# Down projection of an encoder's feed-forward block: one product of full size against seven products of half size

## The chip, the cores and the metric

One core of one Trainium2 chip runs the kernel. The metric is the device time of a run in microseconds (us); lower is better. Engines are named as in the profile: PE (TensorE's matmuls), PEld (its weight loads), DVE (VectorE), ACT (ScalarE), POOL (GpSimd), SP (the engine whose queue issues most DMAs).

## The reference, cut to what matters

The layer is a mixer (attention heads and recurrent heads) followed by a gated feed-forward block. The change is in the last of these, for T = 768 tokens (512 of `x_sample`, then 256 of `x_prompt`), D = 1024, D_FF = 2816, all float32:

```python
def _conv_ffn(xn, w_gate, w_up, conv_w, conv_b, w_down):
    a = xn @ w_gate
    a = lax.conv_general_dilated(a, conv_w[:, None, :], ...) + conv_b   # depthwise, 3 taps along the tokens
    b = xn @ w_up
    return (jax.nn.gelu(a, approximate=True) * b) @ w_down              # <- the down projection

# y = h + RMSNorm_post2(_conv_ffn(RMSNorm_pre2(h), ...))
```

## The kernel before

A product in float32 precision is made from three float32r matmuls: each operand is split into a high part (an ACT copy, line 242) and a low part (a DVE subtraction, line 243; helper `split_to`), and hi·hi, lo·hi and hi·lo are added in PSUM.

**Gate and up.** The gate and up projections are already made by seven half-size products (the names P1 to P7; A11, A12, ... are halves of the tokens' operand, B11, ... halves of the weights). A pair p is a column tile f and its partner f + 11 of one of the two weight matrices (even p gate, odd p up). For every pair `prep` makes the weights' combinations (line 828, DVE) and splits them, six products ahead of `product` (line 844, 12 matmuls of 384 columns for each product). `keep` and `collect` take the results out of PSUM into CG (gate) or CU (up), `gate` runs the convolution and GELU into UM, and `gated` multiplies by up (line 895) and stores the gated tile of 128 features to `Gd` in DRAM (lines 896 and 897, SP). Weights come through a ring of five raw buffers (RAW and EX), loaded at line 228 on SP.

**Down.** `run` ends with the down projection, out of `Gd` and `w_down`. It has two halves of 512 output columns. In each, for each f of 22 feature tiles, six token tiles of 128 take three matmuls of 512 columns (line 1149): 2 x 22 x 6 x 3 = 792. One PSUM bank holds one token tile. Gated tiles are loaded (line 1122, 384 KB each, every one twice) into four buffers in X and split three tiles ahead into XN2; weights are loaded in pieces of 512 KB and split. The last f's (4 in the first half, 6 in the second) run token tile by token tile, so that each token tile's norm (lines 1173 to 1176 in the first half, 734 to 737 in the second), residual (line 1185) and store (line 1187) lie beside the next tile's matmuls, but for the last one.

**What sets the order.** SP's and POOL's instructions run in the order of the program. Those of PE, DVE and ACT are ordered by the scheduler when the program is built, and each engine then runs its list in order.

Of the kernel before, what the change touches and what calls it, by code (L numbers as in the profile page):

```python
# [6 lines left out]
F32 = mybir.dt.float32  # L7
# [3 lines left out]
OP = mybir.AluOpType  # L11

D = 1024
# [29 lines left out]
H = T // 2  # L43

# [48 lines left out]
class Encoder:  # L93
# [80 lines left out]
    def weight_list(self):  # L174
# [27 lines left out]
        wd = a["w_down"][0].rearrange("(k p) c -> p k c", p=128)  # L202
        for half in range(2):
            for s in range(NF // 2):
                L.append((wd[:, s:s + NF // 2 + 1:NF // 2, 512 * half:512 * half + 512], 2, 512))
# [608 lines left out]
    def prep(self, upto):  # L814

        nc = self.nc
        while self.n_op < min(upto + 1, len(self.prods)):
# [13 lines left out]
            if kind == "P4":  # L831
                self.n_split = n + 2
                self.load(n + 7)

# [58 lines left out]
    def gated(self, f, c, u):  # L893
        nc = self.nc
        nc.vector.tensor_tensor(self.v(u, T + 1), self.v(u, T + 1), self.v(c, T + 1), op=OP.mult)
        nc.sync.dma_start(self.Gd[f, :, 0:SA], self.v(u, SA))
        nc.sync.dma_start(self.Gd[f, :, SA:T], self.v(u + SA + 1, SB))

    def run(self):
        nc, ps = self.nc, self.ps  # L900
        self.weight_list()
        self.Gd = self.tc.dram_tile([NF, 128, T], F32, name="gd")
        self.Hd = self.tc.dram_tile([T, D], F32, name="hd")
# [114 lines left out]
        for f in range(7):  # L1018
# [10 lines left out]
            if f == 0:  # L1029
# [8 lines left out]
                                                   ("S3", self.X + 16 * H))}  # L1038

# [67 lines left out]

        n1 = N_FFN + 2 * NF
        order = [f + x for f in range(NF // 2) for x in (0, NF // 2)]
        GS, GR, HR = self.XN2, self.X + 9216, self.X  # L1110
        M0, M1 = self.V, self.V + 3072
        banks = ((0, 3, 5, 6, 7, 2), (1, 4, 0, 3, 5, 6))
        LATE = (4, 6)
        n_l = n_g = 0

        def gs(n):
            return GS + 1536 * (0, 1, 4, 5, 2, 3)[n % 6]

        def gload(upto):
            nonlocal n_l  # L1120
            while n_l < min(upto, 2 * NF):
                nc.sync.dma_start(self.v(GR + T * (n_l % 4), T), self.Gd[order[n_l % NF]])
                n_l += 1

        def gsplit(upto):
            nonlocal n_g
            while n_g < min(upto, 2 * NF):
                gload(n_g + 1)
                o = gs(n_g)
                self.split_to(o, o + T, GR + T * (n_g % 4), T)  # L1130
                n_g += 1
                gload(n_g + 4)

        for m in range(4, len(self.prods)):
            self.prep(m)
            self.product(m)
            self.keep(m)
            p, kind = self.prods[m]
            if p == NF - 1:
                {"P1": lambda: gload(4), "P6": lambda: (gsplit(2), self.split(n1 + 1)), "P3": lambda: gsplit(4),  # L1140
                 "P7": lambda: self.split(n1 + 2)}.get(kind, lambda: None)()
            self.collect(m)
            self.prep(m + 6)
        def down(half, f, i):
            m = n1 + 11 * half + f // 2
            wh, wl = self.hi(m) + 512 * (f % 2), self.lo(m) + 512 * (f % 2)
            o = gs(half * NF + f)
            for go, wo_, first, last in ((o, wh, True, False), (o + T, wh, False, False), (o, wl, False, True)):
                nc.tensor.matmul(ps[:, banks[half][i], :], self.r(go + 128 * i, 128), self.r(wo_, 512),  # L1149
                                 start=(f == 0 and first), stop=(f == NF - 1 and last))  # L1150

        ss0 = {}
        self.split(n1 + 4)
        for half in range(2):
            late = NF - LATE[half]
            for f in range(late):
                gsplit(half * NF + f + 3)
                for i in range(NTT):
                    down(half, f, i)
                if f % 2:  # L1160
                    self.split(n1 + 11 * half + f // 2 + 4)
            if half == 0:
                for i in range(NTT):
                    nc.sync.dma_start(self.v(HR + 1024 * i, 1024), self.Hd[128 * i:128 * i + 128, :])
            gsplit((half + 1) * NF)
            for i in range(NTT):
                for f in range(late, NF):
                    down(half, f, i)
                out = ps[:, banks[half][i], :]
                h, m0 = HR + 1024 * i, M0 + 512 * i  # L1170
                if half == 0:
                    ss = self.col()
                    nc.scalar.activation(self.v(self.JUNK, 512), out, AF.Square, accum_out=ss)
                    nc.vector.tensor_tensor(self.v(m0, 512), out, self.v(self.WB, 512), op=OP.mult)
                    ss0[i] = self.col()
                    nc.vector.tensor_scalar(ss0[i], ss, D * EPS, None, op0=OP.add)
                    if i == 2:
                        gsplit(NF + 2)
                    continue
                m1 = M1 + 512 * (i % 4)  # L1180
                rs = self.post_stats(ss0[i], out, self.v(m1, 512))
# [42 lines left out]
```

## Time and profile before

| | |
|---|---|
| median of 3 runs | 1028.98 us (1028.87 to 1029.11) |
| the profiled execution's own time | 1028.98 us |
| its span (first to last instruction) | 1027.2 us |
| mean clock granted to TensorE | 0.992 of full speed |
| PE busy | 996.8 us, 97% of the span |
| DVE busy, ACT busy | 651.8 us, 498.3 us |
| gate and up products, without the first four | 524 to 840.5 us of the span |
| down projection's matmuls | 840.5 to 1020.2 us |

Read it from the top: the engine that is busy nearly always, then the stretch of the span in which each part of the program runs, then what each of the other engines does in that stretch. The profiled execution lasted as long as the median run, and 1.8 us of its time lie outside the span. A matmul's duration in the profile is longer than the distance to the next one, since matmuls are pipelined; busy time divided by count gives the distance.

### The profile page before, as it was taken

The page shows a single profiled execution, that of the slowest core. Times are in us where ns is not written, and L with a number is a line of the kernel's source. Part 1 is how long each engine was busy: PE and PEld are TensorE (multiplying, and loading weights), DVE is VectorE, ACT ScalarE, POOL GpSimd, SP SyncE. Part 2 cuts the span into 40 slices and gives each one's busy share as a digit, 9 for nine tenths or more (in the row PEclk, how much of TensorE's full clock was granted, in tenths as well). Part 3 has the DMA queues.
Part 4 walks back from the last instruction along what each step waited for, and adds up shares of the span by engine and source line. Part 5 has one row for each costly group of instructions (what it writes and reads, how often), then busy time and mean ns, then how long its engine had stood idle before and what let it go on. Part 6 is the DMA issues. An engine that isn't in the chain of part 4 may idle for free.

```text
span 1027.2 us, 17503 instructions
## 1 busy us (share of the span) xinstructions
PE 996.8 (97%) x7087; PEld 888.9 (87%) x7087; DVE 651.8 (63%) x1106; ACT 498.3 (49%) x901; POOL 49.4 (5%) x45
## 2 busy tenths in 40 slices
PE   5999999999989999999979999999999999999997
PEld 5988888888878777779879999999999998888885
DVE  5445949494623677636899777887777673345334
ACT  4363535252414889735656455555544563334321
POOL 1100000000022011001100000000000000000001
PEclk9999999999989999999989999999999999999999
DMA  9041111111024122142345233233332466474313
GB/s 276 24 124 44 43 42 42 42 43 42 3 69 119 44 58 57 29 144 83 129 121 151 74 112 97 74 104 107 113 113 75 137 223 212 153 276 156 132 41 123
DMA packets 109874, 104.01 MB, mean 101 GB/s; under 512 B 4602, under 2 KB 89698, under 8 KB 109794
## 3 DMA queue, kind: packets, MB, share of 16 engines
q1 hardware_dynamic: 108930, 101.33, 31.9%
q10 hardware_dynamic: 864, 1.57, 0.4%
q8 instruction: 55, 0.90, 0.4%
q14 instruction: 25, 0.20, 0.1%
HBM read 85.58 MB, written 14.94 MB: 98 GB/s over the span
## 4 chain that ended last, share of the span: by engine, by line
PE 86%; issue 6%; DVE 3%; ACT 2%; POOL 1%; DMA 1%; SPq 0%; DVEq 0%; POOLq 0%; ACTq 0%
PE ps L844 31%; PE ps L338 19%; PE ps L1149 17%; PE ps L710 4%; PE ps L346 4%; PE ps L430 2%; PE ps L630 2%; PE ps L663 2%; PE ps L652 2%; PE ps L515 1%; DMA RAW<-w_in 1%; PE ps L512 1%; DVE XN L796 1%; DVE V L747 0%; POOL sm L526 0%
## 5 line engine op out<-in xcount | busy, mean ns | idle before, releaser
L338 PE MATMUL ps<-X,W 128*128 128x512 f32 (+1 forms) x1200 | 232.5, 345 | 0.0
L338 PEld LDWEIGHTS ps<-X,W 128*128 128x128 f32 x1200 | 187.2, 190 | 28.0 <-issue 2.4
L844 PE MATMUL ps<-XN,W 128*128 128x384 f32 x1056 | 189.8, 337 | 5.4 <-ACT XN L795 4.6
L844 PEld LDWEIGHTS ps<-XN,W 128*128 128x128 f32 x1056 | 184.9, 189 | 6.4 <-ACT XN L795 5.4
L1149 PE MATMUL ps<-W,XN 128*128 128x512 f32 x792 | 179.7, 389 | 0.0
L1149 PEld LDWEIGHTS ps<-W,XN 128*128 128x128 f32 x792 | 148.7, 188 | 30.8
L242 ACT ACTIVATE W<-RAW 128x1024 fp32r<-128x1024 f32 (+1 forms) x92 | 79.7, 869 | 175.9 <-PE ps L338 75.6
L844 PE MATMUL ps<-X,W 128*128 128x384 f32 x792 | 144.2, 340 | 0.0
L844 PEld LDWEIGHTS ps<-X,W 128*128 128x128 f32 x792 | 140.8, 189 | 0.0
L243 DVE TENSOR_TENSOR W<-RAW,W 128x512 fp32r<-128x512 f32 (+1 forms) x82 | 78.1, 955 | 66.0 <-ACT W L242 65.9
L242 ACT ACTIVATE W<-V 128x512 fp32r<-128x512 f32 x88 | 55.1, 628 | 59.0 <-PE ps L844 56.0
L243 DVE TENSOR_TENSOR W<-V,W 128x512 fp32r<-128x512 f32 x88 | 59.8, 688 | 17.8 <-ACT W L242 17.7
L346 PE MATMUL ps<-W,X 128*128 128x256 f32 (+1 forms) x432 | 66.6, 312 | 3.3 <-ACT X L804 2.5
L346 PEld LDWEIGHTS ps<-W,X 128*128 128x128 f32 x432 | 61.7, 196 | 4.9 <-ACT X L804 3.1
L243 DVE TENSOR_TENSOR XN<-X,XN 128x768 fp32r<-128x768 f32 x44 | 41.8, 955 | 35.8 <-ACT XN L242 35.7
L242 ACT ACTIVATE XN<-X 128x768 fp32r<-128x768 f32 x44 | 36.8, 840 | 42.8 <-PE ps L1149 42.6
L710 PE MATMUL ps<-W,X 128*128 128x512 f32 (+1 forms) x288 | 57.2, 343 | 0.0
L710 PEld LDWEIGHTS ps<-W,X 128*128 128x128 f32 x288 | 44.1, 188 | 6.9 <-issue 1.6
L242 ACT ACTIVATE W<-EX 128x512 fp32r<-128x512 f32 (+1 forms) x34 | 25.3, 745 | 47.5 <-PE ps L1149 22.5
L243 DVE TENSOR_TENSOR W<-EX,W 128x512 fp32r<-128x512 f32 (+1 forms) x34 | 28.2, 830 | 29.6 <-ACT W L242 29.6
L304 POOL TENSOR_TENSOR sm<-sm 128x1 f32<-128x1 f32 x24 | 15.2, 639 | 622.1 <-DVE sm L735 587.7
L860 ACT ACTIVATE V<-ps 128x384 f32<-128x384 f32 x66 | 31.4, 475 | 6.3 <-PE ps L844 6.3
(183 smaller groups left out, 1151.8 us busy)
## 6 DMA issues: line engine op xcount, KB each, us to landing
X<-gd SPq DMA_DIRECT2D x44, 384.0 KB
RAW<-w_in SPq DMA_DIRECT2D x32, 512.0 KB
RAW<-w_gate SPq DMA_DIRECT2D x14, 512.0 KB
RAW<-w_up SPq DMA_DIRECT2D x13, 512.0 KB
RAW<-w_down SPq DMA_DIRECT2D x13, 512.0 KB
gd<-UM SPq DMA_DIRECT2D x22, 256.0 KB
EX<-w_up SPq DMA_DIRECT2D x9, 512.0 KB
EX<-w_down SPq DMA_DIRECT2D x9, 512.0 KB
```

The source lines that it names most:

```text
L242: nc.scalar.activation(self.r(hi, n), self.v(src, n), AF.Copy)
L243: (eng or nc.vector).tensor_tensor(self.r(lo, n), self.v(src, n), self.v(hi, n), op=OP.subtract)
L338: nc.tensor.matmul(out, self.r(wo + 128 * k, 128), self.r(xo + T * k + t0, tn), start=(k == 0 and first), stop=(k == NK - 1 and last))
L346: self.nc.tensor.matmul(out, self.r(xo + T * k + 128 * i, 128), self.rap(wo + 128 * k, [[1024, tiles], [1, 128]]), start=(k == 0 and first ...
L430: nc.tensor.matmul(ps[64 * cb:64 * cb + 64, b + h, 64 * c:64 * c + 64], self.v(kt + t0, 64, *HALF[h]), qv(t0, h), start=True, stop=True)
L630: nc.tensor.matmul(ps[:, 4 + h, 0:L], self.r(QS + T * h + t0 + 128 * i, 128), self.r(x + T * h + t0, L), start=z, stop=not z)
L652: nc.tensor.transpose(ps[:, 6 + h, 128 * kt:128 * kt + 128], ms(j, n, h)[:, 128 * kt:128 * kt + 128], self.ident)
L663: nc.tensor.matmul(o[64 * h:64 * h + 64], self.v(vb + 128 * kt + 64 * h, 64), self.v(pt(s, h) + L * kt, L), start=kt == 0, stop=kt == L // ...
L710: nc.tensor.matmul(out, self.r(mo + T * f + 128 * i, 128), rhs, start=(f == 0 and first), stop=(f == NK - 1 and last))
L844: nc.tensor.matmul(out, self.r(wo + 128 * k, 128), self.r(xo + H * k, H), start=kind in BEGINS and k == 0 and first, stop=k == 3 and last, ...
L860: self.nc.scalar.activation(self.v(o, H), self.ps[:, self.pair_banks(p)[BANK_OF[kind]], 0:H], AF.Copy)
L1149: nc.tensor.matmul(ps[:, banks[half][i], :], self.r(go + 128 * i, 128), self.r(wo_, 512), start=(f == 0 and first), stop=(f == NF - 1 and ...
```

## The change

The down projection is made the way gate and up are made: the token half (384 tokens), the feature half (11 tiles) and the column half (512) are combined so that seven products of half size in each dimension replace eight. `UNITS` lists 77 units in four stages of 22, 22, 22 and 11: (P1, P5), (P6, P3), (P7, P2), (P4), one unit for each product and feature tile f of 11. A unit is 3 token tiles x 3 matmuls of 512 columns (line 1012): 77 x 9 = 693. Banks are kept from stage to stage (P6, P7 and P4 add to what P1 left there, P3 to what P5 left), so that a stage's result is copied out (line 1071, ACT) or added to a block in V (line 1050, DVE) where it ends.

The tokens' sums (S1 to S4) are made where the gated tiles are made, in `token_sums`: for each f below 11, seven DVE instructions (lines 912 to 917) and six stores to a new DRAM tensor `Sd`. The second halves of those `Gd` tiles are no longer stored. Gated operands are loaded as 192-KB pieces (line 960, six buffers), weights as 256-KB pieces (line 949, ten buffers, and eleven places in X for B12, which is first copied from `w_down` to a DRAM tensor `Bd`, line 835, one piece for each second pair). `down_prep` works six units ahead and subtracts weights on DVE (lines 985, 991, 996) in 44 of the 77 units.

```diff
+UNITS = [(k, f) for ks in (("P1", "P5"), ("P6", "P3"), ("P7", "P2"), ("P4",)) for f in range(NS) for k in ks]
...
             if kind == "P4":
                 self.n_split = n + 2
                 self.load(n + 7)
+                if p % 2:
+                    nc.sync.dma_start(self.Bd[p // 2], self.wd[:, p // 2, 512:1024])
...
-        nc.sync.dma_start(self.Gd[f, :, 0:SA], self.v(u, SA))
-        nc.sync.dma_start(self.Gd[f, :, SA:T], self.v(u + SA + 1, SB))
+        nc.sync.dma_start(self.Gd[f, :, 0:H], self.v(u, H))
+        if f >= NS:
+            nc.sync.dma_start(self.Gd[f, :, H:SA], self.v(u + H, SA - H))
+            nc.sync.dma_start(self.Gd[f, :, SA:T], self.v(u + SA + 1, SB))
+        else:
+            self.token_sums(f, u, self.UM + NG * ((2 * f + 1) % 4), c, c + NG)
+
+    def token_sums(self, f, a1, a2, c0, c1):
...
+        for o, t, m in pieces:
+            nc.vector.tensor_tensor(self.v(s1 + t, m), self.v(a1 + o, m), self.v(a2 + o, m), op=OP.add)
+        nc.vector.tensor_tensor(self.v(s2, H), self.v(s1, H), self.v(a1, H), op=OP.subtract)
+        for o, t, m in pieces:
+            nc.vector.tensor_tensor(self.v(c0 + o, m), self.v(a1 + t, m), self.v(a1 + o, m), op=OP.subtract)
+        for o, t, m in pieces:
+            nc.vector.tensor_tensor(self.v(c1 + o, m), self.v(a2 + t, m), self.v(s2 + t, m), op=OP.subtract)
+        nc.sync.dma_start(self.Sd[f, :, 0:H], self.v(s1, H))
...
+    def down_prep(self, upto, cap=1000):
...
+            src, x, y = {"P5": (t, 0, 1), "P7": (self.V + 3072 + 1024 * (f % 3), 0, 1)}.get(k, (None,) * 3)
+            if k == "P6":
+                src = t
+                nc.vector.tensor_tensor(self.v(t, 512), self.v(raw[0], 512), self.v(t, 512), op=OP.subtract)
...
+            w, g = self.down_ops(u)
+            self.split_to(w, w + 4096, src, 512)
+            self.split_to(g, g + H, self.X + 9216 + H * (u % 6), H)
+            if k == "P2":
+                nc.vector.tensor_tensor(self.v(t, 512), self.v(raw[0], 512), self.v(t, 512), op=OP.subtract)
...
+            self.down_g(u + 7)
...
+    def down_product(self, u, tiles):
...
+        for i in tiles:
+            for go, wo, first, last in ((g, w, True, False), (g + H, w, False, False), (g, w + 4096, False, True)):
+                nc.tensor.matmul(self.down_bank(k, i), self.r(go + 128 * i, 128), self.r(wo, 512),
...
+    def down(self):
...
+        late = 6
...
+        for u in range(n - late):
+            k, f = UNITS[u]
+            self.down_prep(u)
+            self.down_product(u, range(N))
+            if f == NS - 1:
+                if k in ("P1", "P5", "P6"):
+                    for i in range(N):
+                        nc.scalar.activation(self.down_block(*{"P1": (i, 0), "P5": (i + N, 1), "P6": (i, 1)}[k]),
+                                             self.down_bank(k, i), AF.Copy)
+                else:
+                    for i in range(N):
+                        add(*{"P3": (i, 1), "P7": (i + N, 1), "P2": (i, 0)}[k], k)
...
+            self.down_prep(u + 6)
...
+        for i in range(N):
+            for u in range(n - late, n):
+                self.down_product(u, (i,))
...
+            out = self.down_bank("P4", i)
+            rs = self.rsqrt(self.down_square(i + N, 0, out, ss[i + N]))
+            self.down_weigh(i + N, 0, out)
+            self.down_store(i + N, rs)
```

**DVE beside gate and up**, from the second gated product of a tile f to the next use of new raw weights (W is the split weights, CU and UM the up and gated tiles, V the combined weights). Before:

```order
L895 TENSOR_TENSOR UM<-UM,CU 128x769 [waits DVE_49,Activation_49]
L243 TENSOR_TENSOR W<-V,W 128x512 [waits PE_49,Activation_49] x2
L828 TENSOR_TENSOR V<-EX,RAW 128x512 [waits DMAHW7_49,DMAHW4_49]
L243 TENSOR_TENSOR W<-RAW,W 128x512 [waits PE_49,Activation_49]
L828 TENSOR_TENSOR V<-EX,V 128x512 [waits DVE_49]
```

and in the changed kernel:

```order
L897 TENSOR_TENSOR UM<-UM,CU 128x769 [waits DVE_49,Activation_49]
L912 TENSOR_TENSOR CU<-UM 128x128 [waits DVE_49]
L912 TENSOR_TENSOR CU<-UM 128x256
L915 TENSOR_TENSOR CU<-UM 128x128
L913 TENSOR_TENSOR CU<-CU,UM 128x384 [waits DVE_49]
L915 TENSOR_TENSOR CU<-UM 128x256
L917 TENSOR_TENSOR CU<-UM,CU 128x128 [waits DVE_49]
L917 TENSOR_TENSOR CU<-UM,CU 128x256
L243 TENSOR_TENSOR W<-V,W 128x512 [waits PE_49,Activation_49] x2
L243 TENSOR_TENSOR W<-RAW,W 128x512 [waits PE_49,Activation_49]
```

The seven sums stand in one block ahead of the next low parts.

**SP at the same place**: the stores of the gated tile and the loads of weights that are queued behind them. Before:

```order
L896 DMA gd<-UM 128x512 [waits DMAHW2_49,DVE_49]
L897 DMA gd<-UM 128x256 [waits DMAHW3_49]
L228 DMA EX<-w_gate 128x8x128 [waits DMAHW4_49,Activation_49]
L228 DMA EX<-w_up 128x8x128 [waits DMAHW5_49]
L228 DMA RAW<-w_up 128x8x128 [waits DMAHW6_49,DVE_49]
```

and in the changed kernel:

```order
L898 DMA gd<-UM 128x384 [waits DMAHW5_49,DVE_49]
L918 DMA sd<-CU 128x384 [waits DMAHW6_49,DVE_49]
L919 DMA sd<-CU 128x384 [waits DMAHW7_49,DVE_49]
L922 DMA sd<-CU 128x128 [waits DMAHW0_49]
L922 DMA sd<-CU 128x256 [waits DMAHW1_49,DVE_49]
L922 DMA sd<-CU 128x128 [waits DMAHW2_49,DVE_49]
L922 DMA sd<-CU 128x256 [waits DMAHW3_49,DVE_49]
L228 DMA RAW<-w_gate 128x8x128 [waits DMAHW4_49,Activation_49]
L228 DMA EX<-w_up 128x8x128 [waits DMAHW5_49]
```

Six stores in place of one now wait for DVE ahead of the weights' loads.

**DVE in the down projection**, between two weight splits of one half before (XN_4144 holds the split gated operands, X the raw ones):

```order
L243 TENSOR_TENSOR W<-RAW,W 128x1024 [waits PE_49,Activation_49]
L243 TENSOR_TENSOR XN_4144<-X,XN_4144 128x768 [waits DMAHW7_49,Activation_49]
L243 TENSOR_TENSOR XN_4144<-X,XN_4144 128x768 [waits DMAHW1_49,Activation_49]
L243 TENSOR_TENSOR W<-RAW,W 128x1024 [waits PE_49,Activation_49]
L243 TENSOR_TENSOR XN_4144<-X,XN_4144 128x768 [waits DMAHW2_49,Activation_49]
```

and in the third stage of the changed kernel, one unit of P2 and one of P7 (X also holds B12, V and UM the weights' differences):

```order
L243 TENSOR_TENSOR W<-RAW,W 128x512 [waits PE_49,Activation_49]
L243 TENSOR_TENSOR XN_4145<-X,XN_4145 128x384 [waits DMAHW3_49,Activation_49]
L243 TENSOR_TENSOR W<-V,W 128x512 [waits PE_49,Activation_49]
L243 TENSOR_TENSOR XN_4145<-X,XN_4145 128x384 [waits DMAHW5_49,Activation_49]
L991 TENSOR_TENSOR V<-RAW,X 128x512 [waits DMAHW2_49,DVE_49]
L996 TENSOR_TENSOR UM<-RAW,UM 128x512 [waits DMAHW0_49]
```

One round was three subtractions for 36 matmuls; it is six smaller ones for 18.

## Rows read from the trace of the kernel before

**Rows 1.** The page: span, busy time of PE, and the chain that ended last

```profile
span 1027.2 us, 17503 instructions
PE 996.8 (97%) x7087; PEld 888.9 (87%) x7087; DVE 651.8 (63%) x1106; ACT 498.3 (49%) x901; POOL 49.4 (5%) x45
...
PE 86%; issue 6%; DVE 3%; ACT 2%; POOL 1%; DMA 1%; SPq 0%; DVEq 0%; POOLq 0%; ACTq 0%
```

**Rows 2.** Groups of the page: line, count, busy us, mean ns

```profile
L1149 PE MATMUL ps<-W,XN 128*128 128x512 f32 x792 | 179.7, 389 | 0.0
```

**Rows 3.** Busy time in stretches: columns, gate and up, down, the end

```profile
core 0: us, PE busy (x) PEld busy (x) DVE busy (x) ACT busy (x) POOL busy (x), PEclk, DMA share, GB/s
524.00:840.50 316.50, 316.50 (x1799) 316.50 (x1799) 250.88 (x400) 173.12 (x309) 0.00 (x0) 0.99 0.39 117
840.50:1020.20 179.70, 179.70 (x794) 148.54 (x792) 75.25 (x92) 57.81 (x81) 2.75 (x5) 1.00 0.45 158
880.00:920.00 40.00, 40.00 (x178) 33.15 (x177) 15.06 (x16) 13.36 (x17) 0.00 (x0) 1.00 0.58 207
1020.20:1027.20 7.00, 0.04 (x1) 0.00 (x0) 2.22 (x4) 0.69 (x2) 0.55 (x1) 0.82 0.30 112
```

**Rows 4.** Groups by shape, 420 to 1028 us: nearest to the added work

```profile
L243 DVE TENSOR_TENSOR W<-V,W 128x512 fp32r<-128x512 f32 x88 | 59.8, 688 | 17.8 <-ACT W L242 17.7
L242 ACT ACTIVATE W<-V 128x512 fp32r<-128x512 f32 x88 | 55.1, 628 | 59.0 <-PE ps L844 56.0 <-DVE V L828 3.0
L860 ACT ACTIVATE V<-ps 128x384 f32<-128x384 f32 x66 | 31.4, 475 | 6.3 <-PE ps L844 6.3
L880 DVE TENSOR_TENSOR CU<-ps,V 128x384 f32<-128x384 f32 x22 | 12.2, 556 | 4.1 <-PE ps L844 4.1
L880 DVE TENSOR_TENSOR CU<-ps,V 128x256 f32<-128x256 f32 x11 | 4.6, 416 | 0.0
L880 DVE TENSOR_TENSOR CU<-ps,V 128x128 f32<-128x128 f32 x11 | 3.2, 292 | 7.4 <-PE ps L844 7.4
```

**Rows 5.** Waits of PE, then ACT, 524 to 1028 us: total, times, longest

```profile
PE ps L844 <- DVE XN L796: 0.7, 1, 0.7
...
ACT W L242 <- PE ps L844: 104.1, 94, 1.5
```

**Rows 6.** Busy time in stretches beside gate and up, columns as in 3

```profile
531.00:546.00 15.00, 15.00 (x88) 15.00 (x87) 14.39 (x24) 12.28 (x21) 0.00 (x0) 1.00 0.59 173
561.00:576.00 15.00, 15.00 (x88) 15.00 (x87) 14.62 (x24) 8.38 (x15) 0.00 (x0) 1.00 0.27 75
681.00:711.00 30.00, 30.00 (x173) 30.00 (x173) 23.10 (x38) 16.00 (x30) 0.00 (x0) 1.00 0.37 105
```

**Rows 7.** Timeline, 705 to 732 us: start, us, engine, instruction [idle before]

```profile
724.53 0.96 DVE L895 TENSOR_TENSOR UM<-UM,CU 128x769 f32<-128x769 f32 x1
726.00 0.69 DVE L243 TENSOR_TENSOR W<-V,W 128x512 fp32r<-128x512 f32 x1 [0.51 <-ACT W L242]
728.14 0.69 DVE L243 TENSOR_TENSOR W<-V,W 128x512 fp32r<-128x512 f32 x1 [1.45 <-ACT W L242]
730.64 0.69 DVE L828 TENSOR_TENSOR V<-EX,RAW 128x512 f32<-128x512 f32 x1 [1.81 <-DMA EX<-w_gate]
...
726.41 0.40 SPq L228 DMA_DIRECT2D EX<-w_gate  x1
```

**Rows 8.** Timeline of PE, 505 to 531 us, and busy time behind its wait

```profile
522.52 0.44 PE L844 MATMUL ps<-XN,W 128*128 128x384 f32 x1 [4.56 <-ACT XN L795]
...
524.00:528.00 4.00, 4.00 (x14) 4.00 (x14) 3.82 (x7) 1.67 (x4) 0.00 (x0) 0.50 0.12 30
```

**Rows 9.** DMA issues of the page into X and of w_down: count, KB

```profile
X<-gd SPq DMA_DIRECT2D x44, 384.0 KB
...
RAW<-w_down SPq DMA_DIRECT2D x13, 512.0 KB
...
EX<-w_down SPq DMA_DIRECT2D x9, 512.0 KB
```

More of the change, by code (lines that the diff above doesn't have):

```diff
@@ L43 @@
 H = T // 2
+NS = NF // 2
+UNITS = [(k, f) for ks in (("P1", "P5"), ("P6", "P3"), ("P7", "P2"), ("P4",)) for f in range(NS) for k in ks]
 TILES = (0, 1, 3, 2, 4, 5)
@@ L201, in weight_list @@
                     L.append(cols(src, 128 * x))
[L202 to L205, printed above, removed]
         self.wl = L
@@ new lines, in down_setup @@
+    def down_setup(self):
+        self.n_dp = self.n_dg = self.n_dw = self.n_used = 0
+        self.raws = [("B12", 0), ("B11", 0), ("B11", 1), ("B11", 2)]
+        for f in range(1, NS):
+            self.raws += [("B12", f)] + ([("B11", f + 2)] if f + 2 < NS else [])
+        self.raws += [("B22", f) for f in range(NS)]
+        for f in range(NS):
+            self.raws += [("B22x", f), ("B21", f)]
+        ring = [x for x in self.raws if x[0] != "B12"]
+        self.ring = {x: i for i, x in enumerate(ring)}
@@ new lines, in raw_at, with down_w @@
+    def raw_at(self, x):
+        if x[0] == "B12":
+            return self.X + (11520 if x[1] == 0 else 512 * (x[1] - 1))
+        i = (4 * NF + self.ring[x]) % 10
+        return (self.RAW + 1024 * ((N_FFN + i // 2) % 3) if i < 6 else self.EX + 1024 * (i // 2 - 3)) + 512 * (i % 2)
+    def down_w(self, upto):
+        while self.n_dw < min(upto, len(self.raws)):
+            x = self.raws[self.n_dw]
+            k, c = {"B11": (0, 0), "B21": (NS, 0)}.get(x[0], (NS, 1))
+            self.nc.sync.dma_start(self.v(self.raw_at(x), 512), self.Bd[x[1]] if x[0] == "B12" else
+                                   self.wd[:, k + x[1], 512 * c:512 * c + 512])
+            self.n_dw += 1
@@ L1106, in run @@
         self.collect(3)
[L1108 to L1134, printed above, removed]
+        self.down_setup()
+        n = len(self.prods)
+        for m in range(4, n):
             self.prep(m)
@@ L1137, in run @@
             self.keep(m)
[L1138 to L1141, printed above, removed]
             self.collect(m)
             self.prep(m + 6)
[L1144 to L1181, printed above, removed]
-                y = self.a["y_sample"][0, 128 * i:128 * i + 128] if i < 4 else \
-                    self.a["y_prompt"][0, 128 * (i - 4):128 * (i - 4) + 128]
-                for c, src, eng in ((0, m0, nc.sync), (512, m1, nc.scalar)):
-                    nc.vector.scalar_tensor_tensor(self.v(src, 512), self.v(src, 512), rs, self.v(h + c, 512),
-                                                   op0=OP.mult, op1=OP.add)
-                    eng.dma_start(y[:, c:c + 512], self.v(src, 512))
-            if half == 0:
-                self.split(n1 + 11 + 4)
@@ L1191, in bcast @@
+            if m == n - 6:
+                self.down_g(6)
+                self.down_w(4)
+            if m >= n - 6:
+                self.down_prep(m + 6 - n, {n - 6: 4, n - 5: 14}.get(m, 1000))
+        self.down()
     def bcast(self, name):
```

98 lines of the change are left out of this document (added).

## The prediction

> **What bounds the kernel now.** First the page: PE is busy for 996.8 of 1027.2 us and holds 86% of the chain that ended last [rows 1]. Then the groups, for what the down projection is made of: 792 matmuls of line 1149 in 179.7 us, 0.2269 us from one to the next, with no idle time ahead of them [rows 2]. Then busy time in stretches, for what the other engines have to spare in each part. Beside gate and up PE is busy all the time and DVE for 250.88 of 316.5 us; in the down projection PE is busy for 179.70 of 179.70 us, DVE for 75.25, ACT for 57.81, the 16 DMA engines for 0.45 of it [rows 3]. Last the waits: PE waits once for DVE there, 0.7 us, while ACT waits for PE 94 times, 104.1 us in all, since the next place in the ring of split weights is still in use [rows 5]. So in both parts PE alone sets the pace and the preparation runs as far ahead as its buffers let it. A matmul taken out here shortens the span by its distance, for as long as the preparation keeps up.
>
> **What is taken out.** 792 matmuls become 77 x 9 = 693 of the same shape and in the same pattern, three for a token tile with the high part loaded twice. 99 x 0.2269 = 22.5 us less; the down projection would last 693 x 0.2269 = 157.2 us. The Trainium skill (TensorE: Matmul & The Clock Gate, section "Wait — 56ns, not 53.3ns?") gives a warm matmul of N columns N / 2.4 GHz and some 2.5 ns, which would be 215.8 ns for 512 and an estimate of 21.4 us for the 99; the trace has 226.9 ns, and the row decides.
>
> **What is added beside gate and up.** For each f of 11, seven DVE sums: three of 128 elements, three of 256, one of 384. The nearest rows are line 880's 292, 416 and 556 ns [rows 4]: 3 x 0.292 + 3 x 0.416 + 0.556 = 2.68 us, 29.5 us for eleven. Bounds: nothing, where DVE's spare time takes them, and 29.5 us, where DVE is the bound throughout. I take nothing. In the steady part DVE is busy for 23.10 of each 30 us [rows 6]; a tile f takes 2 x 7 x 12 matmuls, 168 x 316.5 / 1799 = 29.6 us, so the sums raise DVE from 77% to 86%. The tightest place is the start: from 531 to 576 us, in three windows of 15 us, DVE is busy for over 95% (first and last of the three in [rows 6]), and the first sums fall there. PE nevertheless keeps its pace in them (88 matmuls in 15 us, 173 in 30 us later), and low parts are made several products of 2.1 us ahead of their use, so that one delay of 2.7 us uses up part of the lead and no more.
>
> **SP** carries the new stores ahead of the weights' loads. DVE waits for such a load even now: a gated product starts at 724.53 us, the load behind its stores is issued at 726.41, and DVE, having nothing else to do, waits 1.81 us until 730.64 for its data, 4.2 us after the issue [rows 7]. The new stores wait for sums that DVE makes one after another, and all but the last one can go out meanwhile; the load then goes out some 2.7 us later, but DVE comes to its wait 2.7 us later too. The wait keeps its size. The eleven copies into Bd (256 KB each) and 11 x 4 x 192 KB of sums, less 11 x 192 KB not stored to Gd, add 9.4 MB written and 2.9 MB read to a stretch in which the DMA engines are busy for 0.39 [rows 3]: nothing.
>
> **What is added in the down projection.** All of it lies beside matmuls. A unit is 9 x 0.2269 = 2.04 us of PE. DVE's low part of 512 weights takes 0.69 us; that of 384 gated columns lies between 0.56 (from PSUM) and 0.69, I take 0.56; a subtraction of weights takes 0.69 [rows 4]. A pair of units is 4.08 us of PE and on DVE 3.2 us in the first and second stages (five operations), 3.9 us in the third (six: 4 x 0.69 + 2 x 0.56); a unit of the fourth is 1.25 of 2.04 us. ACT has 2 x (0.63 + 0.5) = 2.3 us in a pair, 0.5 being my estimate for 384 elements from 0.475 out of PSUM. DVE, which had 100 us to spare, becomes nearly full, but stays under PE in every stage. The third is the tightest: it opens with three additions and three weighings of finished blocks (6 x 0.69 = 4.1 us) and then leaves 0.2 us in each pair. What covers them is the lead of six units, 12.2 us. Of the nine ACT copies and nine additions that free banks, each has at least one unit of 2.04 us until its bank is written again, against 3 x 0.6 or 3 x 0.69 us of work: nothing, or up to 0.1 us at each of three stage ends.
>
> **The way in.** The first six units are prepared within the last six products of gate and up, in buffers that these products free. DVE's load of the last pair stays about the same: eight operations of 768 or 1024 columns go, fifteen smaller ones come. P5's second and later differences need B12 in a part of X that P6 of the last pair still reads; its load starts four products (8 us) before the end, takes some 4.2 us, and is needed three units in. I take nothing. If it fails, the price is that of a wait of this size in the trace: PE waited 4.56 us before 522.52, and in the 4 us behind that the granted clock was 0.50, which is the level of 1.2 GHz; 14 matmuls passed where 23 pass at 2.4 GHz [rows 8], so 4.6 + 9 x 0.176 = 6.2 us.
>
> **Loads.** Before, 44 gated loads of 384 KB and 22 of weights of 512 KB [rows 9]; now 77 of 192 KB and 55 of 256 KB: 29.6 MB against 28.8, in twice as many transfers. Bounds: by bytes, a first or third stage asks for 44 loads, 10.1 MB in 22 x 2.04 = 44.9 us, or 225 GB/s, where the engines gave 207 at 0.58 [rows 3], so 0.63 and nothing to pay. By count, 0.45 x 179.7 us went to 66 loads, 6 of the residual and 12 stores, 0.96 us each; the third stage with its 50 would take 48 us, 3.3 more than PE. I take the first: the pieces within a load stay at 1.5 and 2 KB, and gate and up move 117 GB/s at 0.39, 300 GB/s at full use, with less regular traffic. Here a rule speaks against the change: the Trainium skill (DMA: Bandwidth & Descriptors, section "Bandwidth") wants DMAs of 1 MiB or more for 75% of peak, from measurements of single transfers on another queue. Were it to hold, the smaller pieces would cost by count, and the sum would be 3.3 us worse; the trace, with 207 GB/s out of 384 and 512 KB at 0.58, speaks for the bytes.
>
> **The end** stays: the last token tile's 18 matmuls, then square, norm, two residual steps and a store, 7.0 us after the last matmul [rows 3].
>
> **Sum**, against the profiled execution's own 1028.98 us, which is also the median of the runs: 1028.98 - 22.5 = **1006.5 us**.
>
> **Rivals.**
> *DVE in the third stage.* If the engine makes each difference, waits for ACT's high part and only then the low part, a pair costs 0.69 + 0.63 + 0.69 + 0.56 + 1.94 = 4.51 us against 4.08: 11 x 0.43 = 4.7 us, with the opening 4.1 us, is 8.8 us behind. With the lead of 12.2 us none of it shows; with none, 1015.3. Half of it is 1011. For it: DVE is as good as full. Against it: the order puts differences three units ahead, so that ACT is not waited for. Chance 0.15, for 1008.5 to 1015.3.
> *Loads or the way in.* 3.3 us by count in the third stage, and one wait of 4.6 us with the low clock behind it, 6.2 us: 1016. For it: some data are asked for only 4 us ahead. Against it: six gated and ten weight buffers are 12 and 20 us of lead. Chance 0.07.
> *Slower: the sums at their full price.* If DVE becomes the bound beside gate and up, 29.5 us stand against the 22.5 saved: 1036. It decides where a tile's 22.8 us of DVE work, 2.7 of sums and its waits for data exceed the 29.6 us of PE, that is, once those waits pass 4.1 us for each f. For it: DVE is the fullest engine after PE, and one wait of 1.81 us is in the rows. Against it: in the steady part its idle time is mostly waits for free places [rows 5]. Chance 0.04.
> That the change doesn't do what it says is no rival: the order of PE's instructions has 693 rows of the new line.
>
> **How the numbers follow.** The forecast has 0.74, with a range of its own from 1005.3 (the last store's landing is part of the 7.0 us at the end and may be shorter) to 1008.5 (0.1 us at each of three stage ends, and small waits of the sizes in [rows 5, 7], 0.7 and 1.81 us). Adding the rival of the third stage takes the range to 1014, with 0.87 in it; as the lead may be smaller than I read it, I leave it there, a little over eight in ten. Faster 0.94: all but the sums' rival and a small part in which several prices add up; within 0.2%, which is 2 us and about what a measurement of this kernel can tell from no change, 0.02; slower 0.04.
>
> **What would show it.** Right: 693 matmuls of 512 columns in about 157 us without idle time ahead of them; gate and up again 316 us long, with DVE near 88% there; DVE over 80% of the down projection; 7 us after the last matmul. Wrong: waits of PE for DVE in the third stage, for DMA at the start of a stage, a granted clock under 1 at the way in, or fewer matmuls in each 15 us beside gate and up.

## The result and the profile after

The changed kernel takes 1006.8 us (median of 4 runs, 1005.73 to 1007.12), the one before 1028.92 (4 runs, 1027.98 to 1029.11). The ratio is 0.9782, with a 95% interval from 0.9771 to 0.9794: 22.1 us less, where 22.5 had been forecast. The profiled execution of the changed kernel took 1005.73 us, the lowest of the four, with a span of 1003.9.

The page of the changed kernel, its span, its engines and the chain that ended last, beside [rows 1]:

```profile
span 1003.9 us, 17989 instructions
PE 973.4 (97%) x6988; PEld 868.5 (87%) x6988; DVE 722.4 (72%) x1324; ACT 525.2 (52%) x998; POOL 52.2 (5%) x45
...
PE 83%; issue 7%; DVE 4%; ACT 2%; DMA 1%; POOL 1%; SPq 1%; DVEq 0%; POOLq 0%; ACTq 0%
```

PE is still 97% of the span, and still the chain. DVE rose by 70.6 us and ACT by 26.9 in a span that is 23.3 us shorter. Whether this work is hidden is read from the idle time ahead of PE's groups, 522 us to the end (line, count, busy us and mean ns, idle before and its releasers), beside [rows 2]:

```profile
L1012 PE MATMUL ps<-W,XN 128*128 128x512 f32 x693 | 157.3, 389 | 0.0
L846 PE MATMUL ps<-X,W 128*128 128x384 f32 x792 | 144.1, 339 | 0.3 <-ACT V L862 0.3
```

The 693 matmuls of the down projection wait for nothing; those of gate and up wait once more than before, for 0.3 us. Now busy time in stretches (the columns of [rows 3]): gate and up; the down projection, whole and by its four stages; the end; the first 12 us of the down projection by themselves; and three stretches of [rows 6] again.

```profile
522.80:840.10 317.30, 316.99 (x1799) 316.42 (x1800) 270.62 (x476) 172.42 (x315) 0.00 (x0) 0.99 0.46 139
840.10:997.20 157.10, 157.10 (x695) 129.97 (x693) 126.66 (x234) 85.47 (x172) 5.61 (x5) 1.00 0.60 200
840.10:885.00 44.90, 44.90 (x200) 37.20 (x199) 41.47 (x79) 27.03 (x54) 0.00 (x0) 1.00 0.80 266
885.00:930.00 45.00, 45.00 (x200) 37.26 (x200) 31.72 (x57) 25.97 (x50) 0.00 (x0) 1.00 0.57 179
930.00:975.00 45.00, 45.00 (x200) 37.29 (x199) 36.23 (x66) 26.05 (x55) 0.00 (x0) 1.00 0.60 203
975.00:997.20 22.20, 22.20 (x99) 18.23 (x98) 17.25 (x35) 6.42 (x16) 5.61 (x5) 1.00 0.28 105
997.20:1003.90 6.70, 0.22 (x1) 0.00 (x0) 2.22 (x4) 0.69 (x2) 0.55 (x1) 0.91 0.34 127
...
840.10:852.00 11.90, 11.90 (x55) 9.84 (x54) 11.90 (x25) 5.65 (x11) 0.00 (x0) 1.00 1.03 369
...
531.00:546.00 15.00, 15.00 (x87) 15.00 (x86) 14.61 (x25) 11.14 (x19) 0.00 (x0) 1.00 0.59 171
561.00:576.00 15.00, 15.00 (x88) 15.00 (x87) 15.00 (x26) 9.20 (x17) 0.00 (x0) 1.00 0.38 115
680.00:710.00 30.00, 30.00 (x174) 30.00 (x173) 25.25 (x45) 16.20 (x31) 0.00 (x0) 1.00 0.45 134
```

PE is busy in every microsecond of all four stages, beside a DVE that is busy for 126.66 of 157.1 us. The first stage is the fullest for the others: DVE 41.47 of 44.9 us, the DMA engines 0.80 of it at 266 GB/s. These are averages: in its first 12 us DVE has no gap at all and the DMA engines are full (a share of 1.03) at 369 GB/s, and PE still waits for nothing. Beside gate and up DVE has 19.7 us more to do than in [rows 3], 2.0 for each of the ten f whose sums lie there (the eleventh's are made at 843 us, in the down projection). The first sums run from 551 to 553 us, and from 561 to 576 us no gap at all is left in DVE; PE passes its 88 matmuls in these 15 us all the same. The end is 6.7 us.

The new wait of 0.3 us lies in the way in. The chain of waits there (start us, us, what):

```profile
813.36 0.47 DVE CU L913
...
814.22 0.44 SPq L922
...
819.25 0.43 SPq L960
...
819.72 1.16 SPq L949
820.93 4.94 DMA EX<-w_down
...
826.51 0.83 ACT UM L893
...
829.11 0.39 ACT V L862
829.53 10.77 PE ps L846 x60
```

and ACT's wait for a load in it (total, times, longest, us):

```profile
ACT W L242 <- DMA EX<-w_down: 2.4, 1, 2.4
```

SP stands behind the sums of the tenth f until 814.2 us, then issues their stores, the copy into Bd and six gated loads; the first loads of weights go out from 820 on. (These are the "last sums" of the texts below: the last ones beside gate and up.) ACT, which splits the weights, waits 2.4 us for one, comes late to the copy of line 862, and PE waits for that. It is the one place where the change's new work reached PE.

Where the 23.3 us between the two spans lie: the down projection 179.7 to 157.1, 22.6; the end 0.3; the start of gate and up 0.9 earlier (523.66 and 522.77 us for the first matmul after the wait of [rows 8]; the runs below spread from 522.7 to 524.4 there, so it isn't the change's but this execution's luck); gate and up themselves 0.5 longer, 0.3 of it the new wait.

### The profile page after: what moved, and what is told of

It is laid out like the page before. It is cut to its first block, busy times and chain, and to the rows that moved or that the text cites. A ratio compares the mean times of both kernels' runs of the same rounds, so it can differ in the third digit from the quotient of the medians.

```text
span 1003.9 us, 17989 instructions
## 1 busy us (share of the span) xinstructions
PE 973.4 (97%) x6988; PEld 868.5 (87%) x6988; DVE 722.4 (72%) x1324; ACT 525.2 (52%) x998; POOL 52.2 (5%) x45
## 4 chain that ended last, share of the span: by engine, by line
PE 83%; issue 7%; DVE 4%; ACT 2%; DMA 1%; POOL 1%; SPq 1%; DVEq 0%; POOLq 0%; ACTq 0%
PE ps L846 30%; PE ps L338 20%; PE ps L1012 15%; PE ps L710 5%; PE ps L346 3%; PE ps L430 2%; PE ps L630 2%; PE ps L663 2%; PE ps L652 2%; PE ps L515 1%; DMA RAW<-w_in 1%; PE ps L512 1%; DVE XN L796 1%; POOL sm L304 1%; DMA EX<-w_down 0%
## 5 line engine op out<-in xcount | busy, mean ns | idle before, releaser
L1012 PE MATMUL ps<-W,XN 128*128 128x512 f32 x693 | 157.3, 389 | 0.0
L242 ACT ACTIVATE W<-RAW 128x512 fp32r<-128x512 f32 (+1 forms) x98 | 77.8, 797 | 149.6 <-PE ps L338 74.6
L1012 PEld LDWEIGHTS ps<-W,XN 128*128 128x128 f32 x693 | 130.1, 188 | 26.9
L242 ACT ACTIVATE W<-V 128x512 fp32r<-128x512 f32 x99 | 61.8, 629 | 59.9 <-PE ps L846 46.8
L243 DVE TENSOR_TENSOR W<-V,W 128x512 fp32r<-128x512 f32 x99 | 67.2, 688 | 2.5 <-ACT W L242 2.4
L304 POOL TENSOR_TENSOR sm<-sm 128x1 f32<-128x1 f32 x24 | 18.1, 760 | 597.5 <-DVE sm L1026 478.8
L242 ACT ACTIVATE XN<-X 128x384 fp32r<-128x384 f32 x77 | 38.9, 515 | 11.8 <-DMA X<-sd 8.9
L243 DVE TENSOR_TENSOR XN<-X,XN 128x384 fp32r<-128x384 f32 x77 | 41.9, 553 | 3.6 <-ACT XN L242 3.6
L242 ACT ACTIVATE W<-EX 128x512 fp32r<-128x512 f32 x39 | 24.5, 629 | 31.8 <-PE ps L846 17.6
L243 DVE TENSOR_TENSOR W<-EX,W 128x512 fp32r<-128x512 f32 x39 | 26.8, 688 | 12.9 <-ACT W L242 12.8
```

Of the source, the lines that this page charges most:

```text
L242: nc.scalar.activation(self.r(hi, n), self.v(src, n), AF.Copy)
L243: (eng or nc.vector).tensor_tensor(self.r(lo, n), self.v(src, n), self.v(hi, n), op=OP.subtract)
L304: self.nc.gpsimd.tensor_tensor(r, mean, self.mhalf, op=OP.pow)
L1012: nc.tensor.matmul(self.down_bank(k, i), self.r(go + 128 * i, 128), self.r(wo, 512), start=f == 0 and k in ("P1", "P5", "P2") and first, s ...
```

## The experiments

Theory: PE sets the pace throughout; the change pays 99 x 0.2269 us, and all that it adds lies beside matmuls. The rivals are those of the prediction: the sums cost something, DVE's third stage needs its lead, loads cost by their count, the way in.

**Sums alone.** The kernel before, with its old down projection, makes the sums and stores them in Sd, and nobody reads them.

```diff
         nc.sync.dma_start(self.Gd[f, :, SA:T], self.v(u + SA + 1, SB))
+        if f < NF // 2:
+            self.token_sums(f, u, self.UM + NG * ((2 * f + 1) % 4), c, c + NG)
```

> The kernel before, with the seven sums and six stores added for each f of 11 and the old down projection kept (it reads nothing of them). Theory (DVE takes the sums in its spare time): 1028.9 us, within 0.5 either way, and DVE some 25 of 30 us busy in the steady part. Rival (the sums are on the path): 11 x 2.68 = 29.5 us more, 1058 us; half of it, 1044, where only a part is.

Measured: 1028.83 us beside 1028.34, ratio 1.0003 [0.9993, 1.0012]. Gate and up of this kernel in the view of stretches:

```profile
522.50:839.70 317.20, 317.01 (x1800) 317.01 (x1801) 270.56 (x471) 173.43 (x311) 0.00 (x0) 0.99 0.47 141
```

DVE's busy time and the DMA engines' share are those of the changed kernel, and PE's pace is that of before. So the sums and their stores cost nothing that these runs can tell (the interval is about 1 us to either side), and the gain belongs to the down projection. Where DVE's time for them came from is seen in the changed kernel in its waits for weights. From 590 to 800 us, seven f, before (total, times, longest, us):

```profile
DVE V L828 <- DMA RAW<-w_gate: 7.9, 5, 1.7
DVE V L828 <- DMA EX<-w_gate: 3.3, 2, 1.8
```

and in the changed kernel:

```profile
DVE V L828 <- DMA RAW<-w_gate: 2.9, 5, 0.8
DVE V L828 <- DMA EX<-w_gate: 0.8, 2, 0.5
```

With two smaller ones before, 0.9 and 0.8 us, the waits for loads went from 12.9 to 3.7 us. So of the 14 us of sums in this stretch 9.2 were made in time that DVE had spent waiting for weights, 4.3 in its waits for ACT's high parts (23.5 to 19.2). The place of [rows 7] in the changed kernel (start, us, instruction, idle before):

```profile
723.58 0.95 DVE L897 TENSOR_TENSOR UM<-UM,CU 128x769 f32<-128x769 f32 x1
...
728.26 0.38 SPq L228 DMA_DIRECT2D EX<-w_gate  x1
...
732.59 0.69 DVE L828 TENSOR_TENSOR V<-EX,RAW 128x512 f32<-128x512 f32 x1 [0.48 <-DMA EX<-w_gate]
```

**Sums twice, sums four times.** The changed kernel with the seven sums of an f made two or four times over, to see how much room DVE has.

```diff
         s1, s2 = c0, c1
-        for o, t, m in pieces:
-            nc.vector.tensor_tensor(self.v(s1 + t, m), self.v(a1 + o, m), self.v(a2 + o, m), op=OP.add)
...
+        for _ in range(2):
+            for o, t, m in pieces:
+                nc.vector.tensor_tensor(self.v(s1 + t, m), self.v(a1 + o, m), self.v(a2 + o, m), op=OP.add)
...
```

> The changed kernel with the seven DVE sums made twice, with the same results and stores. DVE was 25.25 of 30 us busy with one set, and a set takes 2.2 us between its starts, so two make 27.4 of 30 us. Theory (spare time is left): 1006.8 us, at most 2 more from the first pairs, where DVE is full already. Rival (one set had used the spare time up, and waits for data hid it): 11 x 2.2 = 24 us more, 1031 us.

> The changed kernel with the sums made four times. A tile f then asks DVE for 22.8 + 4 x 2.2 = 31.6 us of PE's 29.6. Theory: DVE is the bound beside gate and up, 11 x 2.0 = 22 us more with its waits hidden, 1029 us, up to 1045 if its waits for data of some 1.5 us for each f come on top. Rival (the durations overstate what DVE needs, and it still fits): 1007 to 1010 us.

Measured: twice 1008.3 us, ratio 0.9798 [0.9782, 0.9814]; four times 1022.74, ratio 0.9945 [0.9925, 0.9965]. PE's waits, of the kernel with twice the sums:

```profile
PE ps L846 <- ACT V L862: 1.9, 2, 1.6
```

and with four times:

```profile
PE ps L846 <- DVE W L243: 5.4, 10, 0.6
PE ps L1013 <- DVE XN L243: 4.7, 1, 4.7
```

Twice the sums leave the steady part alone, with DVE busy for 27.36 of the 30 us from 680 to 710; what grows is the wait in the way in, from 0.3 to 1.9 us, since SP stands that much longer behind the sums of the tenth f. With four times DVE becomes the bound: PE waits for a low part once for each of ten f, and DVE's gated product comes back in the chain of waits every 30.4 us, of which DVE is busy for 30.1:

```profile
606.63 0.95 DVE UM L897
...
637.02 0.96 DVE UM L897
```

In the changed kernel the same step comes every 29.3 us (the sums of line 913 start at 607.92 and 637.24). The prediction's 29.6 us for an f is an average that takes in the stretch of low clock at the start. Ten f at 1.0 us more and the one wait of 4.7 us in the way in, where SP stands behind the tenth f's sums again (its first gated load goes out at 835.0 us), make most of the 15.9 us lost. At least 22 us more, 1029 us, had been expected: too many. And the sums' price is lower than the durations of the rows gave (2.68 us for seven sums). The 22.8 us of DVE's other work in an f and four times 2.0 us make 30.8, close to the period. So the mechanism of the slower rival, DVE as the bound, is there; it begins between two and four times the work that the change adds.

**A third fewer matmuls.** The down projection without the product of the gated columns' low part, 231 of 693 matmuls, so that PE no longer covers what the other engines do.

```diff
-            for go, wo, first, last in ((g, w, True, False), (g + H, w, False, False), (g, w + 4096, False, True)):
+            for go, wo, first, last in ((g, w, True, False), (g, w + 4096, False, True)):
```

> The changed kernel without the matmuls of the gated low parts in the down projection (231 of 693; the low parts are still made, and their product is left out of the result). PE would need 462 x 0.2269 = 104.8 us there. Theory (DVE, 126.7 of 157.1 us busy, is next behind PE): the down projection takes 127 to 135 us, so 977 to 985 us in all. Rival 1 (the preparation has much more to spare): 52.4 us less, 954 us. Rival 2 (the loads, 0.60 of 157.1 us, or ACT, 85.5 us, with their waits are next): above 990 us.

Measured: 977.39 us, ratio 0.9504 [0.9485, 0.9523], 29.4 us less than the changed kernel where the matmuls alone would give 52.4. Its group of matmuls, and the stretch of its down projection:

```profile
L1012 PE MATMUL ps<-W,XN 128*128 128x512 f32 x462 | 111.8, 400 | 11.1 <-DVE V L1050 4.6 <-ACT W L242 3.4 <-ACT V L1071 1.9
```

```profile
842.90:965.50 122.60, 111.53 (x464) 87.21 (x462) 119.20 (x225) 83.96 (x172) 4.52 (x3) 0.97 0.74 238
```

With less for PE to do the down projection lasts 122.6 us, and DVE is busy for 119.2 of them and waits for the other 3.4: it is what comes next behind PE. (PE's own idle time was 11.1 us; the rest of the stretch beyond 104.8 us is matmuls at a granted clock of 0.97.) The stretch is shorter than the 127 to 135 us expected, as some of DVE's work falls outside it (225 instructions where the changed kernel has 234), and the time is at the low edge of 977 to 985. In the changed kernel PE takes 157.1 us: over the whole the preparation has 34.5 us of room by this run, 30.4 by DVE's busy time of 126.66. By how much each stage has room it does not tell.

**Lead of two units.** Preparation two units ahead instead of six, with four split weights in the ring. The gated loads are asked for where the preparation is, so they come later too.

```diff
-        return self.W + 512 * ((len(self.prods) + u) % 8), self.XN2 + 768 * (0, 1, 2, 3, 8, 9, 10, 11, 4, 5, 6, 7)[u % 12]
+        return self.W + 512 * ((len(self.prods) + u) % (4 if u < 71 else 8)), self.XN2 + 768 * (0, 1, 2, 3, 8, 9, 10, 11, 4, 5, 6, 7)[u % 12]
...
-            self.down_prep(u + 6)
+            self.down_prep(u + 2)
...
```

> The preparation in the down projection runs two units ahead instead of six (4.1 us instead of 12.2), with a ring of four split weights instead of eight. My theory: the lead is what covers the places where DVE has a lump of work, above all the opening of the third stage with its 4.1 us of additions and weighings, and the loads that arrive up to 5 us after their issue. With it cut, PE waits for DVE or ACT at the openings of stages two to four and at some loads: 3 to 10 us longer than the changed kernel, 1010 to 1017 us, with the idle time ahead of line 1012's matmuls, longest just behind 930 us. Rival: DVE and ACT keep pace pair by pair and the lead covers nothing: less than 1 us longer, 1006 to 1008 us, no idle time ahead of line 1012.

Measured: 1007.24 us, ratio 0.9792 [0.9778, 0.9805]: my theory of 3 to 10 us fell. The group of matmuls of this kernel:

```profile
L1012 PE MATMUL ps<-W,XN 128*128 128x512 f32 x693 | 157.6, 389 | 1.3 <-DVE V L1050 1.3
```

and what waited for what from 838 us on:

```profile
ACT XN L242 <- DMA X<-sd: 33.0, 25, 2.4
ACT XN L242 <- DMA X<-gd: 12.0, 14, 4.4
...
PE ps L1012 <- DVE V L1050: 1.3, 1, 1.3
```

ACT now waits 45 us for loads, where it waited 11.6 before the lead was cut, and hardly any of it reaches PE. The single wait of 1.3 us isn't at the third stage's opening but at the fourth's, where DVE had waited 4.2 us behind ACT, and ACT for a load, so that DVE's six additions came late. So a lead of two units, 4.1 us, does nearly all that the lead of six does: the third stage's opening was not the tight place that I had made of it. By time this run can't be told from the changed kernel.

**First loads first.** The first gated loads and three loads of weights go to SP ahead of the stores of the tenth f's sums.

```diff
-            if m == n - 6:
+            if m == n - 18:
                 self.down_g(6)
+                self.down_w(3)
+            if m == n - 6:
                 self.down_w(4)
```

> The first six gated loads and the first three loads of raw weights of the down projection are issued ahead of the last sums' stores, so that they don't stand behind them on SP. My theory: ACT's wait of 2.4 us for a load at 825.97 us goes, and with it PE's wait of 0.31 us at 829.53 in the way in; gate and up last 317.0 instead of 317.3 us and the time is 0.3 us shorter, 1006.3 to 1006.6, too little to be told from no change in the runs, but to be seen in the trace. Rival: the last two gated products are late for a reason of their own (DVE's work ahead of them), and the wait of PE stays at 0.3 us or moves to another line. If the early loads instead delay the stores or another load that is needed first, 1007 to 1010.

Measured: 1005.82 us (5 runs, 1005.14 to 1006.33), ratio 0.9776 [0.9762, 0.9789]. The second group of matmuls of gate and up has no wait any more, nor does ACT wait for a load there:

```profile
L846 PE MATMUL ps<-X,W 128*128 128x384 f32 x792 | 143.4, 338 | 0.0
```

The wait of the way in is thus SP's order, as the theory has it. The median is the lowest of all runs that leave no work out, but the two intervals overlap almost entirely: it can't be told from the changed kernel by time.

**Loads cut in two.** To tell bytes from count, each load of the down projection is made as two: of 64 partitions each on SP (split_loads), the same with the second half on POOL (split_pool), and of half the columns each on SP (split_cols). The diffs show the gated loads; those of weights are cut in the same way.

```diff
...
-            self.nc.sync.dma_start(self.v(self.X + 9216 + H * (self.n_dg % 6), H), src)
+            for p in (0, 64):
+                self.nc.sync.dma_start(self.v(self.X + 9216 + H * (self.n_dg % 6), H, p, p + 64), src[p:p + 64])
```

> Each load of gated columns and of raw weights in the down projection is made as two loads of 64 partitions: twice as many transfers of half the size, same bytes, same pieces of 1.5 and 2 KB. My theory: the DMA engines' time goes by bytes, so their busy share in the first stage stays near 0.80 of 45 us and the time within 1 us of the changed kernel, 1006 to 1008; SP's issues (0.45 us each by the trace, 44 of them in the first stage) double to 40 us of the 45, which still fits. Rival: engine time goes by count of transfers, 0.96 us each: 88 transfers in the first and in the third stage take 84 us each where PE takes 45, so some 40 us longer in each, over 1080 us. A third possibility, SP's issues not fitting beside its waits: 1010 to 1020, with SP the releaser of what PE waits for.

Measured: 1024.79 us, ratio 0.9966 [0.9954, 0.9979]. 18 us are lost, neither 0 nor 80. SP's timeline of this kernel (start, us, issues):

```profile
872.64 1.19 SPq L950 DMA_DIRECT2D RAW<-w_down  x2
873.91 1.19 SPq L962 DMA_DIRECT2D X<-gd  x2
875.19 1.19 SPq L962 DMA_DIRECT2D X<-sd  x2
876.43 1.24 SPq L950 DMA_DIRECT2D RAW<-w_down  x2
```

Two of the changed kernel at the same work:

```profile
889.43 0.33 SPq L949 DMA_DIRECT2D RAW<-w_down  x1
889.81 0.91 SPq L960 DMA_DIRECT2D X<-sd  x2
```

One half takes SP 0.6 us to issue, longer than a whole load (0.33 to 0.45). SP hardly ever stands idle, and a load's two issues take 1.2 us: 44 of them need 54 of the 45 us in the first stage. The third possibility is what happened, at a higher price than I had put on it. What PE waited for, and the first stage:

```profile
PE ps L1014 <- ACT XN L242: 12.4, 9, 5.1
```

```profile
840.10:885.00 44.90, 37.92 (x154) 29.73 (x153) 28.62 (x52) 16.04 (x30) 0.00 (x0) 0.92 0.65 191
```

ACT is late there because it waits for gated loads, 15.7 us in all, while the DMA engines are busy for only 0.65 of the stage; the granted clock was 0.92 in it, so the matmuls behind PE's waits were slower as well. The second run was to take SP out of it:

```diff
...
-            for p in (0, 64):
-                self.nc.sync.dma_start(self.v(self.X + 9216 + H * (self.n_dg % 6), H, p, p + 64), src[p:p + 64])
+            for p, eng in ((0, self.nc.sync), (64, self.nc.gpsimd)):
+                eng.dma_start(self.v(self.X + 9216 + H * (self.n_dg % 6), H, p, p + 64), src[p:p + 64])
```

> As split_loads (each load of the down projection as two of 64 partitions), but the second half is issued by POOL, so that SP issues as many transfers as in the changed kernel. My theory: split_loads lost its 18 us to SP, where one half took 0.59 us to issue and a whole load 0.33 to 0.45; with 0.6 us for each load SP needs 26 of 45 us in the first stage and is no longer late: 1006 to 1009 us, no idle time ahead of the down projection's matmuls, busy share of the DMA engines as in split_loads. Rival: the smaller transfers themselves are what costs (engine time or landing by count), whoever issues them: 1015 to 1025. Third: POOL's issues are slower than SP's and take their place: above 1015, with POOL the releaser of the loads.

Measured: 1022.2 us, ratio 0.9925 [0.9892, 0.9958]; the theory of 1006 to 1009 fell. Its first two stages in the view of stretches:

```profile
840.20:885.00 44.80, 44.21 (x196) 36.63 (x197) 37.16 (x69) 21.33 (x42) 19.22 (x38) 1.00 0.98 253
885.00:930.00 45.00, 40.72 (x171) 33.17 (x170) 27.50 (x50) 22.60 (x47) 15.11 (x30) 0.92 0.55 133
```

The DMA engines are now full in the first stage, at fewer bytes than the changed kernel moves at 0.80: 0.98 / 0.253 = 3.9 us of engine time for a MB where it takes 0.80 / 0.266 = 3.0. PE waits at the ends of the first and second stage for the banks' copies, 4.3 and 4.0 us, as ACT waits 55 us in all for gated loads. POOL's issues take 0.52 us each, so they aren't slow. In split_loads the same halves, all from SP, took 0.65 / 0.191 = 3.4 in that stage. So halving the partitions by itself makes less than half of the step from 3.0 to 3.9; the rest came with the second half on POOL's queue, and why is open.

```diff
...
-            self.nc.sync.dma_start(self.v(self.X + 9216 + H * (self.n_dg % 6), H), src)
+            for q in (0, H // 2):
+                self.nc.sync.dma_start(self.v(self.X + 9216 + H * (self.n_dg % 6) + q, H // 2), src[:, q:q + H // 2])
```

> As split_loads, but each load is cut by columns into two of 128 partitions with pieces of half the length (0.75 and 1 KB), all issued by SP. It tells what sets the price of an issue. Theory: the issue of a load costs by its shape, and one of 64 partitions costs 0.59 us where one of 128 costs 0.33 to 0.45; then SP needs 0.33 to 0.45 us for each of these halves, 88 of them 29 to 40 us of the first stage's 45, and the time is 1007 to 1012 us unless the shorter pieces cost the DMA engines more. Rival: a queue with twice as many transfers in it takes longer for each issue, 0.6 us again: about 1025. If the engine time goes up with the number of pieces, the busy share in the first stage goes from 0.80 towards 1 and the time beyond 1030.

Measured: 1007.44 us (2 runs, 1007.16 and 1007.71), ratio 0.9788 [0.9759, 0.9816]. The group of matmuls and the down projection's stretch of this kernel:

```profile
L1014 PE MATMUL ps<-W,XN 128*128 128x512 f32 x693 | 157.7, 389 | 0.9 <-ACT XN L242 0.9
```

```profile
840.30:997.40 157.10, 156.19 (x689) 128.82 (x689) 127.89 (x233) 86.52 (x173) 5.61 (x5) 1.00 0.66 204
```

This is the run that tells bytes from count. Twice as many transfers with pieces of half the length raise the DMA engines' time in the down projection from 0.60 to 0.66 of 157.1 us, 9.4 us for some 130 more transfers, 0.07 us each. By count it would have been 0.96 each. The time is the changed kernel's within what two runs can tell (about 3 us to either side); the trace shows 0.9 us of waiting. An issue took 0.43 to 0.45 us, like a whole load's, so the 0.6 us of split_loads belong to loads of 64 partitions and not to the number of loads under way.

## Why the prediction was right

- **PE alone sets the pace**: shown by the idle time of 0.0 ahead of the 693 matmuls, and from the other side by the run with a third fewer of them, in which DVE takes over only at 122.6 us. The wait of PE for DVE that is read from [rows 5], 0.7 us, ends at 523.66 us, at the start of gate and up; the down projection had none before the change either.
- **99 x 0.2269 = 22.5 us**: the down projection went from 179.7 to 157.1 us, the 157.2 of the forecast. By the rule of the Trainium skill (TensorE: Matmul & The Clock Gate, section "Wait — 56ns, not 53.3ns?"), an estimate of 215.8 ns for 512 columns, it would have been 149.6; the trace does not agree, with 157.1 / 693 = 0.2267 us again.
- **Sums, nothing**: right, and shown apart from the rest. The upper bound was too high: 2.68 us for each f summed durations of rows, and DVE's busy time rose by 2.0. DVE stood at 270.62 / 317.3 = 85%, not near 88%.
- **SP, the wait keeps its size**: wrong beside gate and up, to the good. Of the two delays set against each other, the load's was right: it went out 4.68 us after the start of the gated product (728.26 and 723.58 us) where it had been 1.88, 2.8 us more for the 2.7 forecast. But DVE came to the wait of [rows 7] 4.2 us later, and the wait fell from 1.81 to 0.48 us, all such waits of seven f from 12.9 to 3.7. So "nothing" was right for another reason than the one given, with room that the prediction had not seen. In the way in the step was wrong as well: it looked at the buffer of B12 and its 8 us, and overlooked that the first loads stand on SP behind the sums of the tenth f, which SP has to wait for. It cost ACT 2.4 us and PE 0.3, and doubled sums made 1.9 of it. "Nothing" was mis-sized by these 0.3 us; the 6.2 us of the rival were not in sight, the granted clock staying at 1.00 through the four stages.
- **DVE in the down projection** over 80%: 126.66 / 157.1 = 81%. That the third stage is the tightest was not borne out by DVE's share: the first is fullest, with 41.47 of 44.9 us against 36.23 of 45. It also makes the last gated product and sums, and DVE works ahead in it: 27 low parts of gated columns in a stage of 22 units. And the rival of the third stage had less behind it than its 0.15: with the lead cut to two units the loss was 1.3 us of PE's time, at another place.
- **Loads by bytes**: right, by the run with half the columns. The size was off: 0.63 at 225 GB/s was forecast for a first or third stage, and the first took 0.80 at 266, as it also fetches what the second needs and stores the last gated products and sums; the third took 0.60 at 203. The rule that was weighed (the Trainium skill, DMA: Bandwidth & Descriptors, section "Bandwidth", transfers of 1 MiB or more for 75% of peak) did not bind: loads of 192 and 256 KB gave 266 GB/s in the first stage, and halves of 96 and 128 KB, cut by columns, no loss that the runs can tell. The 300 GB/s at full use that the prediction worked out were too low: in the first 12 us of the down projection the engines are full, of such loads and the stores of the eleventh f, at 369 GB/s.
- **The end**: 6.7 us for 7.0, inside what the range's low end allowed for.

The sum was 0.3 us low against the median. The terms that were mis-sized, 0.3 us in the way in and 0.3 at the end, are as small as that, and smaller than the spread of the runs, 1.4 us. That the sum met the median to 0.3 us is therefore in part luck; what the trace bears out is the term of the down projection, 22.6 us for 22.5.

## What to carry to other kernels

Where one engine is busy without a gap, its work taken out is worth its distance in the trace, and the work that others get for it is free until their own total, with the waits that are left, passes the covered time. Work put ahead of a wait for a load can use up that wait, as here, where 9.2 of 14 us did. Sum it by stage, and look first at the stage in which a new one and the rest of an old one overlap. Count what a queue in order has to wait for at a seam between two parts: here the first loads of the next part, issued ahead of the stores that wait for the last results, took away a wait of ACT of 2.4 us and one of PE of 0.3. A run that takes work from the bounding engine shows in one look how much room the others have.

## What was not expected of the hardware

- In a row of issues a load of 64 partitions took SP about 0.6 us, one of 128 partitions 0.40 to 0.45, whether of 96 or 256 KB; with gaps between them 0.44 and 0.33. Cutting loads by partitions cost 18 us, by columns 0.6 by the medians, less than two runs can tell.
- Loads of 64 partitions, half of them from POOL, took the DMA engines 3.9 us for a MB in the first stage, against 0.65 / 0.191 = 3.4 for such halves all from SP, 0.78 / 0.234 = 3.3 for loads cut by columns and 3.0 for whole loads. The cause is open.
- Small DVE sums that follow one another take less of DVE than their rows say. By the rows of the changed kernel beside gate and up, seven would be 2.68 us again:

```profile
L913 DVE TENSOR_TENSOR CU<-CU,UM 128x384 f32<-128x384 f32 x10 | 5.5, 552 | 0.0
L917 DVE TENSOR_TENSOR CU<-UM,CU 128x256 f32<-128x256 f32 x10 | 4.2, 422 | 0.0
...
L912 DVE TENSOR_TENSOR CU<-UM 128x128 f32<-128x128 f32 x10 | 2.9, 292 | 0.3
```

The chain gives them 0.47 (384 elements), 0.35 (256) and 0.20 (128) from one to the next, and 3 x (0.35 + 0.20) + 0.47 = 2.1 us; DVE's busy time rose by 2.0 for each f.
